# A third of the weight chunks split by DMA: a casting load, a negating copy and an accumulating load

## The chip, the cores and the metric

The kernel runs on one core of one Trainium2 chip. Its time is the device time of that core, in microseconds (us), as the median of several executions. One more execution is recorded by the hardware profiler, and all durations of single instructions come from that one.

The engines are called PE (TensorE, matrix multiplies; PEld is its weight load), DVE (VectorE), ACT (ScalarE), POOL (GpSimd) and SP (SyncE, which here only issues DMAs). Each takes its own instructions strictly in order, so an instruction that waits holds up what stands behind it. DMAs are issued from SP or POOL.

## The reference

One decoder block over 256 tokens with a model width of 2048, in float32:

```python
xn = rms_norm(h, norm_w[layer])
proj = xn @ w_in[layer]
q, k, v, z_attn, z_ssd, xbc, dt_raw, gate_logits = jnp.split(proj, split_idx, axis=-1)
...
attn = dilated_mixture_attention(q, k, v)
y_attn = (attn * jax.nn.silu(z_attn.astype(jnp.float32))).astype(x.dtype) @ w_attn_br[layer]
ssd = ssd_mixer(xbc, z_ssd, dt_raw, conv_w[layer], conv_b[layer], dt_bias[layer], ...)
y_ssd = ssd.astype(x.dtype) @ w_ssd_br[layer]
...
merged = gates[:, :, 0] * y_attn + gates[:, :, 1] * y_ssd
h = h + merged @ w_out[layer]
return rms_norm(h, final_norm_w)
```

Almost all the arithmetic is the products with the weight matrices. Every weight is read from HBM once and used for 256 tokens.

## The kernel before

A float32 product is made of products of a shorter type, float32r. A weight w is split into two float32r parts, hi = w rounded to float32r, and lo = w - hi. The activations are split in the same way. Most products are then x_hi w_hi + x_lo w_hi + x_hi w_lo: for each 128 x 128 block of weights one matmul of hi against 512 columns (both parts of 256 tokens, line 128) and one of lo against 256 columns (line 129).

The weights come in chunks of 128 partitions x 1024 columns of float32 (512 KB; those of w_v have 768 or 896 columns). The helper `weights` handles one chunk: SP issues its load into a tile `raw` (line 115), ACT makes `hi` by a copy that casts (line 116), and DVE makes `lo` by a subtraction (line 117). `raw` has five buffers, `hi` and `lo` have four each. The helper `project` (lines 120 to 130) calls it for every eight weight blocks, so a chunk is good for 16 matmuls there. `value_product` (lines 205 to 219) and the output blocks (lines 636 to 647) call it too. The last output block has a split of its own (lines 653 to 659), which also takes a `raw` buffer.

PE takes the chunks in the order of the program: values and step sizes, q and k of attention heads, the scan's streams (w_xbc, w_z), the scan's projection (w_ssd), gates (w_gate), w_attn and w_out. Between the chunks stands side work of attention and of the scan, which generators deal out (`step`, `pending`). The tile framework's scheduler sets the order on each engine. `weights` runs under `tc.high_priority`, so loads and splits are placed as early as the buffers permit: with four `hi` buffers, the cast of a chunk waits until PE is done with the chunk four before it.

POOL has little to do: squares of x at the start, constants (lines 318 and 325), one 1 MB load of decay rows for each group of the scan (line 391), residual rows (line 630) and a norm weight.

Of the kernel before, what the change touches and what calls it, by code (L numbers as in the profile page):

```python
# [13 lines left out]
F32 = mybir.dt.float32  # L14
FR = mybir.dt.float32r
# [3 lines left out]
OP = mybir.AluOpType  # L19
PSUM = bass.MemoryType.PSUM  # L20

P = 128
S = 256
# [24 lines left out]
def block_kernel(ctx: ExitStack, tc: tile.TileContext, a: dict, out: bass.AP):  # L48
    nc = tc.nc
    act, dve, pe, sp, pool = nc.scalar, nc.vector, nc.tensor, nc.sync, nc.gpsimd  # L50
# [3 lines left out]
    wts = ctx.enter_context(tc.tile_pool(name="wts", bufs=2))  # L54
# [7 lines left out]
    def ps_main():  # L62
        return ps("mm", 512, 4)
# [10 lines left out]
    def w_tile(name, cols, bufs):  # L74
        return work.tile([P, cols], F32, name=name, bufs=bufs)

    def g1():
        return w_tile("g1", 256, 4)
# [15 lines left out]
    def step(n=2):  # L94
        for _ in range(n):
            if pending:
                try:
                    next(pending[0])
                except StopIteration:
                    pending.pop(0)  # L100
# [2 lines left out]
        while pending:  # L103
            step()

    # ---- weights: load, split into two float32r parts
    def weights(src, parts=1):
        cols = src.free_size()
        with tc.high_priority(offset=100000):
            raw = wts.tile([P, 1024], F32, name="raw", bufs=5)  # L110
            hi = wts.tile([P, 1024], FR, name="hi", bufs=4)
            lo = wts.tile([P, 1024], FR, name="lo", bufs=4)
            for i in range(parts):
                c = slice(i * cols // parts, (i + 1) * cols // parts)
                sp.dma_start(raw[:, c], src[:, c])
                act.copy(hi[:, c], raw[:, c])  # L116
                dve.tensor_sub(lo[:, c], raw[:, c], hi[:, c].bitcast(F32))  # L117
        return hi, lo

    def project(src, rhs, n=KT):  # L120
        """[P channels, 2, S] in PSUM: the product is the sum of the two halves."""
        step()
        pt = ps_main()
        for k in range(n):
            if k % 8 == 0:
                hi, lo = weights(src[:, k:k + 8].rearrange("p k c -> p (k c)"))
            w = slice(k % 8 * P, (k % 8 + 1) * P)
            pe.matmul(pt, hi[:, w], rhs[:, k].rearrange("p a t -> p (a t)"), start=k == 0, stop=False)  # L128
            pe.matmul(pt[:, :S], lo[:, w], rhs[:, k, 0], start=False, stop=k == n - 1)  # L129
        return pt  # L130
# [11 lines left out]
            dve.tensor_add(dst, pt[:, :S], tmp)  # L142

    def silu_half(dst, half):
        """dst = silu(x), from half = x / 2."""
        th = g1()
        act.activation(th, half, AF.Tanh)  # L147
        dve.scalar_tensor_tensor(dst, th, 1.0, half, op0=OP.add, op1=OP.mult)
# [2 lines left out]
        act.copy(dst[:, 0], src)  # L151
        dve.tensor_sub(dst[:, 1], src, dst[:, 0].bitcast(F32))

    # ---- x * norm_w, in two float32r parts; its sum of squares over the model dimension
    with tc.high_priority(offset=100000):
        nw = small("norm_w", sp)
    ones = consts.tile([P, P], F32, name="ones")
    dve.memset(ones, 1.0)
    with tc.high_priority(offset=100000):
        first = consts.tile([P, 1], F32, name="first")  # L160
# [33 lines left out]
        dve.scalar_tensor_tensor(tmp2, tmp2, -0.5, dst, op0=OP.mult, op1=OP.mult)  # L194
        dve.scalar_tensor_tensor(dst, tmp2, 1.5, dst, op0=OP.add, op1=OP.mult)

    # ---- values: tokens on the partitions; the first head slot's carry the scan's step sizes along
    H = SSD_HEADS
    NV = NG * HD

    def apart(v):
        """Tokens in their order, seen as the even ones and the odd ones."""
        return v.rearrange("p (a h) -> p h a", h=2)

    def value_product(src, rhs, n, before=None):
# [29 lines left out]
    for t in range(2):  # L235
        pe.matmul(tot[:, t:t + 1], apart(xsq[:, 0])[:, t], ones[:, :1], start=True, stop=True)
# [4 lines left out]
    def rstd_rows():  # L241
        t = ps_tp()
        for i in range(2):
            pe.matmul(t[:, i * P:(i + 1) * P], rcol[:, i:i + 1].to_broadcast([P, P]), ident, start=True, stop=True)
        act.copy(apart(rstd), t[:, :S].rearrange("p (h a) -> p h a", h=2))
# [59 lines left out]
        act.copy(tok, t[:, :5 * H].rearrange("p (i h) -> p i h", h=H))  # L305
        yield

    # ---- the other constants
    def room(name):
        return consts.tile(list(a[name].shape), F32, name=name + "_sb")  # L310

# [2 lines left out]
    mask = consts.tile([P, 2 * 512], BF, name="mask")  # L314

    def after_start(t):
        """Nothing is loaded into t before the statistics of x are known."""
        pool.tensor_copy(t, rcol[:t.shape[0], 0:1])

    def constants():  # L320
# [9 lines left out]
        act.copy(mask, mask_f)  # L330
        yield

    # ---- rotary angles
    cosb = consts.tile([ROT, S], F32, name="cosb")
    sinb = consts.tile([ROT, S], F32, name="sinb")

# [19 lines left out]
        dve.tensor_scalar(cosb, cosb, -2.0, 1.0, op0=OP.mult, op1=OP.add)  # L356
        yield

    # ---- the scan, one group of eight heads
    sq_sum = consts.tile([P, S], F32, name="sq_sum")  # L360

    def ssd_stream(g):
        xbc = w_tile("six", 6 * S, 2).rearrange("p (i t) -> p i t", t=S)
        for i in range(6):
            ct = g * 4 + i if i < 4 else 32 + (i - 4) * GROUPS + g
            pt = project(a["w_xbc"][ct], xs)
            xc = work.tile([P, S + CONV - 1], F32, name="xc", bufs=2)
            dve.memset(xc[:, :CONV - 1], 0.0)
            evac(xc[:, CONV - 1:], pt)
            acc = g1()  # L370
            act.activation(acc, xc[:, CONV - 1:], AF.Identity, bias=conv_b[:, ct:ct + 1],  # L371
                           scale=conv_w[:, ct, CONV - 1:CONV])
            for j in range(CONV - 1):
                dve.scalar_tensor_tensor(acc, xc[:, j:j + S], conv_w[:, ct, j:j + 1], acc,  # L374
                                         op0=OP.mult, op1=OP.add)
            silu_half(xbc[:, i], acc)
        if g:
            flush()
        zs = w_tile("four", 4 * S, 1).rearrange("p (i t) -> p i t", t=S)
        for i in range(4):  # L380
            pt = project(a["w_z"][8 + g * 4 + i], xs)
            zh = g1()
            evac(zh, pt, scale=0.5)
            silu_half(zs[:, i], zh)
        return xbc, zs
# [72 lines left out]
                                     op0=OP.mult, op1=OP.subtract)  # L458
            yield

    # ---- attention, one head slot of the three groups
    swap = [(i + ROT // 2) % ROT for i in range(ROT)]

    def head_stream(h):
        src = xs if h else xu
        qk = w_tile("six", 6 * S, 2).rearrange("p (i t) -> p i t", t=S)
        waiting = []
        for g in range(NG):
            for i, base in ((g, 0), (NG + g, NG * HEADS)):
                waiting.append((qk[:, i], project(a["w_qk"][base + g * HEADS + h], src)))  # L470
                if h == 0 and len(waiting) == 1 and i == 0:
                    continue
                if h == 0 and i == NG:
                    rstd_rows()
                for dst, pt in waiting:
                    dst = dst.rearrange("p (h a) -> p h a", h=2)
                    tmp = g1()
                    act.copy(tmp, pt[:, S:])
                    if h:
                        dve.tensor_add(dst, apart(pt[:, :S]), apart(tmp))  # L480
                    else:
                        dve.tensor_add(tmp, pt[:, :S], tmp)
                        dve.tensor_mul(dst, apart(tmp), apart(rstd))
                waiting = []
        flush()
        zh = g1()
        evac(zh, project(a["w_z"][h], src), scale=0.5)
        if h == 0:
            dve.tensor_mul(zh, zh, rstd)
        za = w_tile("za", S, 1)  # L490
        silu_half(za, zh)
        v = v0 if h == 0 else values(value_product(a["w_v"][h - 1], xs, NV))
        return qk, za, v
# [44 lines left out]
        split(oT[:, h], oz)  # L538
        yield

    # ---- the SSD branch's projection, half of its inner dimension at a time
    def ssd_project(half):
        for m in range(KT):
            pt = project(a["w_ssd"][half, m], ym)
            tmp = g1()
            act.copy(tmp, pt[:, S:])
            if half:
                dve.tensor_add(ysum[:, m], ysum[:, m], tmp)
                dve.tensor_add(ysum[:, m], ysum[:, m], pt[:, :S])
            else:  # L550
                dve.tensor_add(ysum[:, m], pt[:, :S], tmp)
# [27 lines left out]
    rsqrt_mean(rs, tot2[:, :S], 2 * DM, g1(), g1())  # L579
    ssd_project(1)  # L580

    # ---- gates and merge
    for m in range(KT):
        th = []
        for br in range(2):
# [12 lines left out]
        act.mul(ym[:, m, 0], ya, 0.5)  # L598
        dve.scalar_tensor_tensor(ym[:, m, 1], ya, 0.5, ym[:, m, 0].bitcast(F32), op0=OP.mult, op1=OP.subtract)

    # ---- output projection, residual, final norm
    fw = w_tile("eight", DM, 1)
    every_row(fw, "final_norm_w")
    hres = big.tile([P, 2, DM], F32, name="hres", tag="ysum")
# [28 lines left out]
    for nb in range(NB - 1):  # L633
# [4 lines left out]
        for kk in range(KT):  # L638
            if kk % per == 0:
                hi, lo = weights(a[f"w_out{nb}"][kk // per])  # L640
# [10 lines left out]
    xres = residual(nb)  # L651
    wl = big.tile([P, 2, KT, n], FR, name="wl", tag="xs")
    for i in range(4):
        raw = wts.tile([P, 1024], F32, name="raw", bufs=5)
        sp.dma_start(raw, a[f"w_out{nb}"][i])
        k = slice(4 * i, 4 * i + 4)
        r3 = raw.rearrange("p (k c) -> p k c", k=4)
        act.copy(wl[:, 0, k], r3)
        dve.tensor_sub(wl[:, 1, k], r3, wl[:, 0, k].bitcast(F32))
# [92 lines left out]
```

## Time and profile before

| what | value |
|---|---|
| time, median of 2 runs | 1492.14 us (1491.59 to 1492.70) |
| span of the profiled execution | 1489.9 us |
| PE busy | 1472.8 us, 99% of the span |
| DVE busy | 1036.3 us, 70% |
| ACT busy | 815.6 us, 55% |
| POOL busy | 30.2 us, 2% |
| read from HBM | 275.04 MB, 186 GB/s over the span |
| share of time in which the 16 DMA engines are busy with SP's queue | 53.6% |
| splits of weight chunks on ACT and on DVE | 509 casts, 509 subtractions |

The profiled execution gives no time of its own beside its span; the span is 2.2 us under the median of the runs. A busy PE is no measure of how fast PE is, since matmuls are pipelined. It says only that PE is hardly ever without a matmul under way.

### The profile page before, as it was taken

What the parts mean: (1) busy time and instruction counts of PE and PEld (TensorE: products, weight loads), DVE (VectorE), ACT (ScalarE), POOL (GpSimd) and SP (SyncE); (2) the same over time, 40 slices, a digit from 0 to 9 for tenths busy, and PEclk for the clock granted to TensorE, in tenths of its full rate; (3) what the DMA queues carried; (4) which work ended last, traced back from release to release, by engine and by line L of the source; (5) the groups of instructions that cost most, each with busy time, mean ns of one, the idle gap of its engine ahead of it and who ended that gap; (6) DMA issues with size and microseconds to landing.
All of it is one profiled execution on the core that took longest, in us unless ns stands there. A gap on an engine that the chain in (4) does not pass through costs nothing.

```text
span 1489.9 us, 22408 instructions
## 1 busy us (share of the span) xinstructions
PE 1472.8 (99%) x8581; PEld 1295.7 (87%) x8581; DVE 1036.3 (70%) x1534; ACT 815.6 (55%) x1333; POOL 30.2 (2%) x45
## 2 busy tenths in 40 slices
PE   7999999999999999999999999999999999999997
PEld 6889888888898988888888888999988888888887
DVE  7987777978675654778888775665676666666554
ACT  6654667577544554557575644444454455555444
POOL 4000000000000000000000000000000000000000
PEclk9999999999999999999999999999999999999999
DMA  6656555655554655555555555546555555555563
GB/s 236 216 178 209 183 175 182 208 177 198 174 178 148 234 171 185 192 180 196 175 193 189 192 158 177 189 140 204 199 193 182 190 191 187 195 184 192 191 223 115
DMA packets 79004, 278.67 MB, mean 187 GB/s; under 512 B 9104, under 2 KB 9696, under 8 KB 77744
## 3 DMA queue, kind: packets, MB, share of 16 engines
q1 hardware_dynamic: 76464, 264.81, 53.6%
q0 software_dynamic: 2432, 12.43, 2.5%
q8 instruction: 67, 1.10, 0.3%
q14 instruction: 41, 0.34, 0.1%
HBM read 275.04 MB, written 2.16 MB: 186 GB/s over the span
## 4 chain that ended last, share of the span: by engine, by line
PE 97%; DVE 1%; issue 1%; DMA 0%; ACT 0%; SPq 0%; ACTq 0%; DVEq 0%
PE mm L128 52%; PE mm L129 26%; PE mm L218 3%; PE mm L216 3%; PE mm L217 3%; PE mm L646 2%; PE mm L644 2%; PE mm L645 2%; PE po L534 1%; PE sc L442 1%; DVE xw L185 1%; PE sc L513 0%; PE tp L527 0%; PE tp L407 0%; PE sc L511 0%
## 5 line engine op out<-in xcount | busy, mean ns | idle before, releaser
L128 PE MATMUL mm<-xs,hi 128*128 128x512 f32 x2576 | 911.6, 398 | 0.0
L117 DVE TENSOR_TENSOR lo<-raw,hi 128x1024 fp32r<-128x1024 f32 (+3 forms) x509 | 606.7, 1193 | 374.2 <-ACT hi L116 370.6
L116 ACT CAST hi<-raw 128x1024 fp32r<-128x1024 f32 (+3 forms) x509 | 519.0, 1021 | 501.2 <-PE mm L128 363.0
L129 PE MATMUL mm<-xs,lo 128*128 128x256 f32 x2576 | 719.4, 279 | 0.0
L128 PEld LDWEIGHTS mm<-xs,hi 128*128 128x128 f32 x2576 | 483.6, 188 | 116.1 <-ACT g L147 1.9
L129 PEld LDWEIGHTS mm<-xs,lo 128*128 128x128 f32 x2576 | 485.5, 188 | 0.0
L128 PE MATMUL mm<-ym,hi 128*128 128x512 f32 x512 | 179.8, 397 | 0.0
L129 PE MATMUL mm<-ym,lo 128*128 128x256 f32 x512 | 142.3, 278 | 0.0
L128 PEld LDWEIGHTS mm<-ym,hi 128*128 128x128 f32 x512 | 96.1, 188 | 22.1
L129 PEld LDWEIGHTS mm<-ym,lo 128*128 128x128 f32 x512 | 96.3, 188 | 0.0
L216 PE MATMUL mm<-hi,xs 128*128 128x384 f32 x224 | 75.3, 336 | 0.0
L217 PE MATMUL mm<-lo,xs 128*128 128x384 f32 x224 | 75.3, 336 | 0.0
L218 PE MATMUL mm<-hi,xs 128*128 128x384 f32 x224 | 75.3, 336 | 0.0
L374 DVE SCALAR_TENSOR_TENSOR g<-xc,conv_w_sb,g 128x256 f32<-128x256 f32 x144 | 69.5, 482 | 4.1 <-ACT g L371 1.3
L147 ACT ACTIVATE g<-g 128x256 f32<-128x256 f32 x88 | 36.5, 415 | 19.1 <-DVE g L139 12.8
L644 PE MATMUL mm<-hi,ym 128*128 128x512 f32 (+1 forms) x128 | 46.4, 363 | 0.0
L646 PE MATMUL mm<-hi,ym 128*128 128x512 f32 (+1 forms) x128 | 46.4, 363 | 0.0
L645 PE MATMUL mm<-lo,ym 128*128 128x512 f32 (+1 forms) x128 | 46.4, 362 | 0.0
L128 PE MATMUL mm<-oT,hi 128*128 128x512 f32 x128 | 45.1, 394 | 0.0
L216 PEld LDWEIGHTS mm<-hi,xs 128*128 128x128 f32 x224 | 43.5, 194 | 0.3
L217 PEld LDWEIGHTS mm<-lo,xs 128*128 128x128 f32 x224 | 43.5, 194 | 0.0
L218 PEld LDWEIGHTS mm<-hi,xs 128*128 128x128 f32 x224 | 43.5, 194 | 0.0
(226 smaller groups left out, 1324.0 us busy)
## 6 DMA issues: line engine op xcount, KB each, us to landing
raw<-w_qk SPq DMA_DIRECT2D x96, 512.0 KB, 4.3
raw<-w_xbc SPq DMA_DIRECT2D x96, 512.0 KB, 3.7
raw<-w_z SPq DMA_DIRECT2D x80, 512.0 KB, 3.8
raw<-w_ssd SPq DMA_DIRECT2D x64, 512.0 KB, 3.6
raw<-w_gate SPq DMA_DIRECT2D x64, 512.0 KB, 3.5
raw<-w_v SPq DMA_DIRECT2D x56, 384.0 KB, 3.1
raw<-w_out SPq DMA_DIRECT2D x32, 512.0 KB, 4.2
eight<-cs_rows POOLq DMA_DIRECT2D x8, 1024.0 KB, 6.8
```

Source lines behind the costliest of these rows:

```text
L116: act.copy(hi[:, c], raw[:, c])
L117: dve.tensor_sub(lo[:, c], raw[:, c], hi[:, c].bitcast(F32))
L128: pe.matmul(pt, hi[:, w], rhs[:, k].rearrange("p a t -> p (a t)"), start=k == 0, stop=False)
L129: pe.matmul(pt[:, :S], lo[:, w], rhs[:, k, 0], start=False, stop=k == n - 1)
L147: act.activation(th, half, AF.Tanh)
L216: pe.matmul(pv[t][:, :n], x_hi[:, t], hi[:, w], start=kk == 0, stop=False)
L217: pe.matmul(pv[t][:, :n], x_hi[:, t], lo[:, w], start=False, stop=False)
L218: pe.matmul(pv[t][:, :n], x_lo[:, t], hi[:, w], start=False, stop=kk == KT - 1)
L374: dve.scalar_tensor_tensor(acc, xc[:, j:j + S], conv_w[:, ct, j:j + 1], acc, op0=OP.mult, op1=OP.add)
L644: pe.matmul(po[t][:, :n], ym[:, kk, 0, tk], hi[:, w], start=kk == 0, stop=False)
L645: pe.matmul(po[t][:, :n], ym[:, kk, 0, tk], lo[:, w], start=False, stop=False)
L646: pe.matmul(po[t][:, :n], ym[:, kk, 1, tk], hi[:, w], start=False, stop=kk == KT - 1)
```

## The change

`weights` counts its calls. On every third call, if the chunk is whole (one part, 1024 columns), it takes two other tiles, `hi_acc` and `lo_acc`, of two buffers each, and makes the two parts in another way:

- POOL issues a DMA from the weights in HBM straight into `hi_acc`; the source is float32 and the destination float32r, so the DMA casts.
- ACT writes `lo_acc` = -`hi_acc`.
- POOL issues a second DMA from the same weights in HBM, which adds into `lo_acc`. The result is w - hi.

Such a chunk has no `raw` tile, no load on SP, and no instruction on DVE. Its weights are read from HBM twice. The built program has 150 such chunks: 150 loads fewer stand on SP, and 300 DMAs more on POOL. The other chunks go the old way, with three buffers instead of five for `raw`, and three instead of four for `hi` and for `lo`.

```diff
+    count = [0]
+
     def weights(src, parts=1):
         cols = src.free_size()
+        count[0] += 1
         with tc.high_priority(offset=100000):
-            raw = wts.tile([P, 1024], F32, name="raw", bufs=5)
-            hi = wts.tile([P, 1024], FR, name="hi", bufs=4)
-            lo = wts.tile([P, 1024], FR, name="lo", bufs=4)
+            if parts == 1 and cols == 1024 and count[0] % 3 == 0:
+                hi = wts.tile([P, 1024], FR, name="hi_acc", bufs=2)
+                lo = wts.tile([P, 1024], FR, name="lo_acc", bufs=2)
+                pool.dma_start(hi, src)
+                act.mul(lo, hi.bitcast(F32), -1.0)
+                pool.dma_start(lo, src, accum_op=OP.add)
+                return hi, lo
+            raw = wts.tile([P, 1024], F32, name="raw", bufs=3)
+            hi = wts.tile([P, 1024], FR, name="hi", bufs=3)
+            lo = wts.tile([P, 1024], FR, name="lo", bufs=3)
...
     for i in range(4):
-        raw = wts.tile([P, 1024], F32, name="raw", bufs=5)
+        raw = wts.tile([P, 1024], F32, name="raw", bufs=3)
```

The rest of the diff removes comments and moves line numbers by about ten: lines 115 to 117 of before are 125 to 127 of after, and the new lines are 116 (first DMA), 117 (negating copy) and 118 (accumulating DMA).

How the instructions stand now is shown at two places. The first is POOL's queue. In before, this is what POOL has left to do from the middle of the first scan groups on: the write of the decay rows to HBM and then one 1 MB load into the tile `eight` for each of the eight groups. The brackets name what a DMA waits for: DMASW is an earlier DMA of POOL, the others are engines.

```order
L297 DMA cs_rows<-four_327 64x256 [waits DMASW4_49,DVE_49]
L391 DMA eight_1932<-cs_rows 128x2048 [waits DMASW5_49,DMASW4_49]
L391 DMA eight_2592<-cs_rows 128x2048 [waits DMASW5_49,DVE_49,DMASW6_49,PE_49,Activation_49]
L391 DMA eight_3254<-cs_rows 128x2048 [waits DMASW6_49,DVE_49,DMASW7_49,PE_49,Activation_49]
L391 DMA eight_3916<-cs_rows 128x2048 [waits DMASW0_49,DVE_49,DMASW7_49,PE_49,Activation_49]
```

POOL's queue in the changed program, between the loads for the second and the third of these groups (`eight_2568` and `eight_3224` there):

```order
L116 DMA hi_acc_2660<-w_xbc 128x1024 [waits DMASW2_49,PE_49]
L118 DMA lo_acc_2661<-w_xbc 128x1024 [waits DMASW4_49,PE_49,Activation_49]
L116 DMA hi_acc_2758<-w_xbc 128x1024 [waits DMASW5_49,PE_49]
L118 DMA lo_acc_2759<-w_xbc 128x1024 [waits DMASW6_49,PE_49,Activation_49]
L116 DMA hi_acc_2877<-w_xbc 128x1024 [waits DMASW7_49,DMASW3_49,PE_49]
L118 DMA lo_acc_2878<-w_xbc 128x1024 [waits DMASW0_49,PE_49,Activation_49]
```

The two DMAs of a chunk follow each other. The first waits for PE (the release of the tile by the chunk that used it before), the second for ACT's negating copy. The first DMA of the next such chunk stands behind that second one.

The second place is ACT's queue in the same stretch of the program. Before (`g1` and `xc` are tiles of the scan's streams, `mm` a product in PSUM):

```order
L116 CAST hi_2762<-raw_2761 128x1024
L116 CAST hi_2784<-raw_2783 128x1024
L141 COPY g1_2656<-mm_2609 128x256
L116 CAST hi_2820<-raw_2819 128x1024
L371 ACTIVATE g1_2659<-xc_2654,conv_b_sb_332,conv_w_sb_331 128x256
L116 CAST hi_2842<-raw_2841 128x1024
```

And now:

```order
L117 ACTIVATE lo_acc_2759<-hi_acc_2758 128x1024
L126 CAST hi_2737<-raw_2736 128x1024
L126 CAST hi_2794<-raw_2793 128x1024
L151 COPY g1_2632<-mm_2585 128x256
L381 ACTIVATE g1_2635<-xc_2630,conv_b_sb_332,conv_w_sb_331 128x256
L157 ACTIVATE g1_2640<-g1_2635 128x256
L126 CAST hi_2816<-raw_2815 128x1024
L117 ACTIVATE lo_acc_2878<-hi_acc_2877 128x1024
```

The negating copy `lo_acc_2759` stands ahead of the cast of the chunk before it (`hi_2737`) and of a copy out of PSUM; both wait on ACT until `hi_acc_2758` has landed.

## The prediction

> **What bounds the kernel now.** I read the page's busy times and its chain of waits first, then the stages, then one stretch of PE's timeline, and last the DMAs. The page:
>
> ```profile
> PE 1472.8 (99%) x8581; PEld 1295.7 (87%) x8581; DVE 1036.3 (70%) x1534; ACT 815.6 (55%) x1333; POOL 30.2 (2%) x45
> ...
> PE 97%; DVE 1%; issue 1%; DMA 0%; ACT 0%; SPq 0%; ACTq 0%; DVEq 0%
> PE mm L128 52%; PE mm L129 26%; PE mm L218 3%; PE mm L216 3%; PE mm L217 3%; PE mm L646 2%; PE mm L644 2%; PE mm L645 2%; PE po L534 1%; PE sc L442 1%; DVE xw L185 1%; PE sc L513 0%; PE tp L527 0%; PE tp L407 0%; PE sc L511 0%
> ```
>
> The chain that ended last is PE for 97% of the span, and of that 93 points (lines 128, 129, 216 to 218, 644 to 646) are products with weight chunks. The stages (the columns are the stretch in us, its length, busy us of each engine with its count, PE's granted clock, the share of the DMA engines, GB/s) say where the rest is:
>
> ```profile
> 0.00:31.00 31.00, 22.84 (x94) 19.45 (x94) 24.31 (x35) 17.24 (x28) 16.88 (x22) 0.94 0.73 248
> ...
> 100.00:485.00 385.00, 385.00 (x2296) 337.40 (x2295) 288.75 (x462) 230.47 (x418) 2.71 (x5) 1.00 0.55 182
> ...
> 1370.00:1478.00 108.00, 108.00 (x587) 93.88 (x587) 60.59 (x73) 49.78 (x69) 2.86 (x4) 1.00 0.55 177
> 1478.00:1490.00 12.00, 3.20 (x27) 3.00 (x25) 4.12 (x16) 3.41 (x8) 0.00 (x0) 0.76 0.47 175
> ```
>
> PE lacks work only in the first 31 us (8 us of it) and in the last 12. From 100 us on it is busy without a gap at a granted clock of 1.00. The change takes no matmul away, so relieving DVE (70%) and ACT (55%) frees nothing that the end waits for. The question is only whether weight chunks still arrive in time. What keeps them in time now is seen in who waits for whom:
>
> ```profile
> DVE lo L117 <- ACT hi L116: 370.6, 328, 4.7
> ...
> ACT hi L116 <- PE mm L128: 363.0, 249, 2.7
> ```
>
> ACT's casts wait for PE to release a buffer (249 times), not for a load: the supply runs as far ahead as the four buffers let it.
>
> PE's pace, from its timeline (start, duration, matmul): two starts of line 128 eight weight blocks apart.
>
> ```profile
> 599.87 0.40 PE L128 MATMUL mm<-xs,hi 128*128 128x512 f32 x1
> ...
> 602.64 0.40 PE L128 MATMUL mm<-xs,hi 128*128 128x512 f32 x1
> ```
>
> A chunk lasts 2.77 us on PE.
>
> **The change part by part.** *Taken away:* 150 subtractions of 1.19 us and 150 casts of 1.02 us, worth nothing, because DVE and ACT do not set the end.
>
> ```profile
> L117 DVE TENSOR_TENSOR lo<-raw,hi 128x1024 fp32r<-128x1024 f32 (+3 forms) x509 | 606.7, 1193 | 374.2 <-ACT hi L116 370.6
> L116 ACT CAST hi<-raw 128x1024 fp32r<-128x1024 f32 (+3 forms) x509 | 519.0, 1021 | 501.2 <-PE mm L128 363.0
> ```
>
> and of one group of activations of the same size:
>
> ```profile
> L419 ACT ACTIVATE eight<-eight 128x1024 f32<-128x1024 f32 x8 | 8.4, 1056 | 0.0
> ```
>
> *Added on ACT:* 150 negating copies at 1.06 us (the last row above), which just replace the casts.
>
> *Added as a chain:* an accumulated chunk passes through four steps that nothing overlaps: the tile's release by PE, the first DMA, the copy, the second DMA. The time allowed for it follows from the buffers. `hi_acc` has two, and every third chunk uses one, so between PE's last matmul on a buffer and its first on the next content lie five other chunks: 5 x 2.77 = 13.9 us, and with the side work among them (97% against 93% of the chain) 13.9 x 97/93 = 14.4 us. Call this B. Let L be the chain's length. If L is under B, PE never notices. If it is over, PE stalls by s at each accumulated chunk; two such stalls lie within one chain, so L = B + 2s, and s = (L - B)/2.
>
> The trace shows no casting and no accumulating DMA. The nearest rows are POOL's plain loads and SP's (size, median us from issue to landing):
>
> ```profile
> raw<-w_xbc SPq DMA_DIRECT2D x96, 512.0 KB, 3.7
> ...
> eight<-cs_rows POOLq DMA_DIRECT2D x8, 1024.0 KB, 6.8
> ...
> cme<-x POOLq DMA_DIRECT2D x3, 512.0 KB, 5.0
> ...
> cme<-mask POOLq DMA_DIRECT2D x1, 512.0 KB, 5.8
> ```
>
> and their spread for SP's chunks and for the 1 MB load (first line `raw`, second `eight`):
>
> ```profile
> DMA to landing us min/median/max: 2.8/3.7/8.8
> ```
> ```profile
> DMA to landing us min/median/max: 5.2/6.8/9.3
> ```
>
> The first DMA moves what a 512 KB load moves: bounds 5.0 and 8.8 us, taken 5.0, the row of its own size and queue. The second must read 512 KB of weights and the 512 KB that it adds to: bounds 5.0 us (if only one read counts) and 9.3 us, the longest 1 MB load. I take 9.3, because the DMA engines get fuller. Their share now, from SP's queue between 100 and 485 us (packets, MB, share of 16 engines):
>
> ```profile
> q1 hardware_dynamic: 18724, 65.28, 51.6%
> ```
>
> 65.28 MB are 124.5 chunks of 524 KB; 0.516 x 385 us / 124.5 = 1.60 us of all 16 engines for a chunk. Three chunks last 3 x 2.77 x 97/93 = 8.7 us on PE. With two plain chunks, a casting load and an add of two reads that is 5 x 1.60 = 8.0 us of 8.7, a share of 0.92 instead of 0.55, where waits in the queues grow.
>
> For the doubled read a rule stands in the Trainium skill, "Collectives: The Full Stack", in the section on the bandwidth ceiling: an add done by DMA costs no time in the adder, but it needs two source reads on one ring, measured there as a ratio of 1.93. No row of this trace has such a DMA; at 1.93 in place of 2 the share would come to 0.91.
>
> Four hops between engines come on top. Where DVE follows ACT the timeline shows 0.03 us (a cast that ends at 602.05, its subtraction at 602.08), but a hop from PE or a DMA isn't shown alone; 0.1 each is my estimate, 0.4 in all.
>
> ```profile
> 601.00 1.05 ACT L116 CAST hi<-raw 128x1024 fp32r<-128x1024 f32 x1 [1.72 <-PE mm L128]
> ...
> 602.08 1.23 DVE L117 TENSOR_TENSOR lo<-raw,hi 128x1024 fp32r<-128x1024 f32 x1 [1.55 <-ACT hi L116]
> ```
>
> L = 5.0 + 1.06 + 9.3 + 0.4 = 15.8 us, s = (15.8 - 14.4)/2 = 0.7 us, and 150 x 0.7 = 105 us.
>
> *The wait on ACT.* The negating copy waits on ACT for the first DMA, and the cast of the plain chunk before it stands behind. This cast's chunk is due four chunks (11.1 us) after the release; first DMA 5.0, copy 1.06, cast 1.05, subtraction 1.23 and hops 0.4 make 8.7. Cover 2.4 us: nothing, as long as the first DMA lands within 7.4 us.
>
> *Fewer buffers for plain chunks.* Three `hi` buffers serve two chunks in three, so a plain chunk's buffer is released three or four chunks before it is due, as with four buffers before. Only w_v's chunks, which are never accumulated, lose one: two chunks remain as cover, against a split of three quarters of 1.02 + 1.19 us. Nothing.
>
> *Start.* Two first DMAs and, after ACT's copies, two second ones now stand ahead of or among the loads of x, and a copy stands ahead of ACT's first cast. Four times 0.52 MB at the 248 GB/s of the first stage is 8.5 us if all of it delays the loads, and nothing if it lies in gaps; the critical start is mostly DVE and its waits, so I take 5. POOL's constants wait behind the third first DMA; they are needed later.
>
> *Sum:* 1489.9 (span) + 2.2 (the median of the runs lies that much above it) + 5 + 105 = 1602 us, rounded to 1600.
>
> **The rivals.**
>
> *The chain fits (not slower).* If the second DMA takes the 1 MB load's median of 6.8 us, L is 5.0 + 1.06 + 6.8 + 0.4 = 13.3, below 14.4: no stalls, 1492 + 5 = 1497 us. It decides up to a second DMA of 8.3 us (L = 14.7, s = 0.17, 25 us, which with the start is 2%). For it speaks that each DMA price above is a median under load; against it the share of 0.92. The Trainium skill, "DMA: Bandwidth & Descriptors", section "Anatomy of one DMA", gives for a DMA issued from POOL a fixed 2.0 us plus bytes over 436 GB/s; this would make 3.2 and 4.4 us, an estimate from that page, and the chain fits with 5 us to spare. The trace's 5.0 and 6.8 us for these sizes are longer, so the page's figure is too short here.
>
> *The DMA engines become the bound.* From 8.7 us for three chunks, 4 x 1.60 us go to two plain chunks and two further units; if casting costs two plain chunks and adding three, 7 x 1.60 = 11.2 us are needed, 2.5 us too many for each of 150: 375 us, 1870 us. Nothing in the trace excludes it, as it has no such DMA. It decides from 5.4 units on.
>
> *ACT's queue starves the plain chunks.* If the first DMA takes SP's longest landing, 8.8 us, the cast behind the copy comes 1.4 us late each time: 150 x 1.4 = 210 us, 1710 us. Against it stands POOL's own 5.0.
>
> That the change doesn't do what it says is no rival: the built program has the 150 chunks. If the casting DMA did not round, `lo` would be zero, and the time the same.
>
> **How the numbers follow.** Two per cent, 30 us, is about what a measurement tells from no change. Chances: the chain a little too long (1523 to 1720 us) 0.38; it fits 0.36; DMA engines as the bound 0.16; ACT's queue 0.08; faster by over 2% 0.02, since only 8 + 9 us of the span are not PE's. Slower is 0.38 + 0.16 + 0.08 = 0.62. The range goes from 1490, as PE's work doesn't shrink, to 1820, which leaves out most of the DMA-bound case and little else.
>
> **What would show it.** If right: PE idle in front of lines 138 and 139, waiting for the DMA into `lo_acc`, some 0.7 us at each accumulated chunk; the second DMA near 9 us to landing and the first near 5; a DMA share about 0.85; DVE's busy time down by 150 x 1.19 = 179 us. It is wrong if PE has no gaps after the start (the chain fits), if the first DMA takes over 7.4 us, or if PE waits for plain `hi` or `lo`.

## The result

The changed kernel takes 1656.71 us (median of two runs, 1651.82 to 1661.61) against 1492.14 us: 1.1103 times as long, with a 95% interval of 1.1025 to 1.1182. The profiled execution has a span of 1650.0 us. The forecast was 1600 us, in a range of 1490 to 1820.

The page of the changed kernel, busy times, then DMA queues, then the chain that ended last:

```profile
PE 1527.4 (93%) x8581; PEld 1318.2 (80%) x8581; DVE 868.2 (53%) x1384; ACT 802.8 (49%) x1333; POOL 241.6 (15%) x345
...
q0 software_dynamic: 45632, 169.74, 44.4%
q1 hardware_dynamic: 54864, 186.15, 31.8%
...
issue 67%; POOL 11%; DMA 10%; PE 10%; ACT 1%; DVE 1%; POOLq 0%; SPq 0%; ACTq 0%
POOL hi_acc L116 5%; POOL lo_acc L118 5%; DMA hi_acc<-w_xbc 4%; PE mm L138 4%; DMA hi_acc<-w_z 2%; PE mm L139 2%; DMA raw<-w_v 2%; PE mm L227 1%; PE mm L228 1%; DMA hi_acc<-w_qk 1%; PE mm L226 1%; PE po L544 0%; DMA lo_acc<-w_qk 0%; DVE lo L127 0%; DMA hi_acc<-w_out 0%
```

PE has fallen from 97% of the chain to 10%. The chain now runs through POOL; "issue" is time for which the profile names no releaser. Between 600 and 650 us, where the chain holds nothing but POOL's DMAs, it is the 7.1 to 9.7 us from a first DMA to the second DMA of the same chunk, that is the landing and the copy. DVE lost 168 us of work and gained nothing for the end. The stretch from 100 to 485 us (the columns as before):

```profile
100.00:485.00 385.00, 358.20 (x2055) 307.20 (x2054) 228.18 (x396) 212.02 (x394) 54.52 (x78) 0.98 0.77 213
```

PE works off 2055 matmul records there in place of 2296, and is idle for 27 us. The loss is spread evenly. The times at which PE has started its n-th matmul, worked out from the two traces and that of a later run (three `hi_acc` buffers, below), in us:

```
matmul      350     1600     3200     4800     6400     last
before     76.1    285.8    556.1    827.9   1099.2   1480.9
after      83.6    317.9    614.9    921.0   1217.0   1641.2
f_hi3      84.1    296.1    573.4    845.2   1126.3   1508.0
```

The start costs 7.5 us; the other 153 come at a steady rate, about 1 us for each of the 150 accumulated chunks.

What PE waits for in the changed kernel, from the list of who waited for whom, is the second DMA:

```profile
PE mm L139 <- DMA lo_acc<-w_xbc: 18.8, 16, 2.7
PE mm L139 <- DMA lo_acc<-w_z: 17.9, 11, 3.6
PE mm L139 <- DMA lo_acc<-w_gate: 14.0, 14, 2.1
```

Added up over the trace, PE is idle for 114 us in gaps of over 0.15 us. 76 us of them end with the landing of a `lo_acc`, 12 us with a plain `hi` or `lo`. Waiting is not the whole loss. PE is also busy for 55 us longer with the same matmuls, and for 62 us of its busy time, in place of 4, the profile shows it at half clock (see the last section). At half speed that is at most 29 us of lost work, an estimate from these two figures.

What POOL's queue looks like when this happens (its timeline: start, duration, instruction, and in brackets the idle time before and what ended it):

```profile
615.50 0.88 POOL L118 DMA_DIRECT2D lo_acc<-w_ssd  x1 [7.58 <-ACT g L556]
616.05 0.87 POOL L116 DMA_DIRECT2D hi_acc<-w_ssd  x1
625.43 0.87 POOL L118 DMA_DIRECT2D lo_acc<-w_ssd  x1 [8.51 <-ACT lo_acc L117]
625.99 0.86 POOL L116 DMA_DIRECT2D hi_acc<-w_ssd  x1
```

and ACT's copy between them:

```profile
624.07 1.06 ACT L117 ACTIVATE lo_acc<-hi_acc 128x1024 fp32r<-128x1024 f32 x1 [4.82 <-DMA hi_acc<-w_ssd]
```

One round: the second DMA of a chunk goes out at 615.50 us, and 0.55 us later, without a wait, the first DMA of the next one. That lands after 8.0 us; the copy starts at 624.07 and ends at 625.13, and the next second DMA goes out at 625.43. A round is 9.9 us, and PE needs 8.7 for the three chunks in it. The time from issue to landing over the run (shortest, median, longest; first `hi_acc`, then `lo_acc`):

```profile
DMA to landing us min/median/max: 4.5/7.3/12.8
```
```profile
DMA to landing us min/median/max: 5.2/5.5/10.2
```

Over the 133 accumulated chunks whose buffer PE released after 100 us, worked out from the trace: the first DMA is issued 0.99 us after PE's release in the mean, and within 1 us after the previous second DMA's issue in 74% of them; landing takes 7.44, the wait for the copy 0.09, the copy 1.06, the hop to POOL 0.32, the second landing 5.98. From release to the last landing this makes 15.9 us. PE takes up the low part within 0.5 us of its landing in 53%. For 75 of the 133 chunks PE had released the tile before the previous second DMA went out, for 58 it released it later.

### The profile page after: what moved, and what is told of

Read it like the earlier page. It is cut to its first block, busy times and chain, and to the rows that moved or that the text cites. A ratio compares the mean times of both kernels' runs of the same rounds, so it can differ in the third digit from the quotient of the medians.

```text
span 1650.0 us, 22481 instructions
## 1 busy us (share of the span) xinstructions
PE 1527.4 (93%) x8581; PEld 1318.2 (80%) x8581; DVE 868.2 (53%) x1384; ACT 802.8 (49%) x1333; POOL 241.6 (15%) x345
## 4 chain that ended last, share of the span: by engine, by line
issue 67%; POOL 11%; DMA 10%; PE 10%; ACT 1%; DVE 1%; POOLq 0%; SPq 0%; ACTq 0%
POOL hi_acc L116 5%; POOL lo_acc L118 5%; DMA hi_acc<-w_xbc 4%; PE mm L138 4%; DMA hi_acc<-w_z 2%; PE mm L139 2%; DMA raw<-w_v 2%; PE mm L227 1%; PE mm L228 1%; DMA hi_acc<-w_qk 1%; PE mm L226 1%; PE po L544 0%; DMA lo_acc<-w_qk 0%; DVE lo L127 0%; DMA hi_acc<-w_out 0%
## 5 line engine op out<-in xcount | busy, mean ns | idle before, releaser
L127 DVE TENSOR_TENSOR lo<-raw,hi 128x1024 fp32r<-128x1024 f32 (+3 forms) x359 | 421.7, 1177 | 415.7 <-ACT hi L126 406.9
L138 PE MATMUL mm<-xs,hi 128*128 128x512 f32 x1704 | 608.5, 399 | 0.0
L139 PE MATMUL mm<-xs,lo 128*128 128x256 f32 x1704 | 477.7, 280 | 0.0
L126 ACT CAST hi<-raw 128x1024 fp32r<-128x1024 f32 (+3 forms) x359 | 358.1, 1002 | 156.0 <-PE mm L138 63.3
L138 PEld LDWEIGHTS mm<-xs,hi 128*128 128x128 f32 x1704 | 321.4, 189 | 76.1 <-issue 1.2
L138 PE MATMUL mm<-xs,hi_acc 128*128 128x512 f32 x872 | 323.6, 406 | 0.0
L139 PEld LDWEIGHTS mm<-xs,lo 128*128 128x128 f32 x1704 | 322.9, 189 | 0.5 <-DVE lo L127 0.3
L139 PE MATMUL mm<-xs,lo_acc 128*128 128x256 f32 x872 | 254.6, 292 | 56.8 <-DMA lo_acc<-w_xbc 18.8
L139 PEld LDWEIGHTS mm<-xs,lo_acc 128*128 128x128 f32 x872 | 169.2, 194 | 73.4 <-DMA lo_acc<-w_xbc 24.8
L138 PEld LDWEIGHTS mm<-xs,hi_acc 128*128 128x128 f32 x872 | 168.0, 193 | 38.1 <-issue 1.0
```

## The experiments

Two limits could set this pace, and in the changed kernel they lie within a microsecond of each other: the release of one of two `hi_acc` buffers by PE (the prediction's chain), and POOL's order, in which a first DMA stands behind the second DMA of the chunk before, which waits for that chunk's first landing and copy. A third theory is that the DMA engines are simply full. All ratios are to the kernel before, with 95% intervals.

**Without the dependency.** The copy reads a constant:

```diff
-                act.mul(lo, hi.bitcast(F32), -1.0)
+                act.mul(lo, ones[:, :1].to_broadcast([P, 1024]), -1.0)
```

> The changed kernel, but ACT's negating copy reads a constant of ones instead of hi_acc, so the second DMA no longer waits for the first one to land (the low part is then w - 1 and not w - hi; every DMA, copy and matmul is still there). POOL's loop: the round loses landing and copy, so it is gone: 1495 to 1530 us. DMA load: the same DMAs, so 1640 to 1665 us. Buffers: the chain gets shorter by the first landing and the copy and fits: 1495 to 1520 us.

Measured: 1502.46 us, 1.007 (1.0055 to 1.0085). Every DMA is still there:

```profile
q0 software_dynamic: 45632, 169.74, 51.3%
q1 hardware_dynamic: 54864, 186.15, 35.9%
```

The engines carry the same packets in less time, at a share of 0.87, and PE is busy for 98% of the span. DMA load is excluded as the cause. The 0.92 that the prediction feared is not far from this, and 0.87 does no harm by itself here. The run does not tell POOL's loop from the buffer chain, since both lose the first landing and the copy.

**A third buffer, first try.** `hi_acc` with three buffers, `raw` with two to make room:

```diff
-                hi = wts.tile([P, 1024], FR, name="hi_acc", bufs=2)
+                hi = wts.tile([P, 1024], FR, name="hi_acc", bufs=3)
...
-            raw = wts.tile([P, 1024], F32, name="raw", bufs=3)
+            raw = wts.tile([P, 1024], F32, name="raw", bufs=2)
```

> The changed kernel with a third buffer for hi_acc (raw gets two instead of three, to make room); POOL's order stays. Three theories. Buffers (the prediction's): the chain of an accumulated chunk starts when PE releases hi_acc. A third buffer lets it start three chunks (8.7 us) earlier, so the stalls go and the time is 1495 to 1520 us. POOL's loop: what starts the first DMA is not the release but POOL's own order, where it stands behind the second DMA of the accumulated chunk before, which itself waits for the first DMA's landing and the copy; a round is first landing 7.7 + copy 1.06 + issues and hops 1.1 = 9.9 us for every 8.7 us of PE's work, whatever the buffers: unchanged, 1640 to 1665 us. DMA load (the engines can't move more): unchanged as well, 1640 to 1665 us.

Measured: 1562.34 us, 1.0473 (1.0456 to 1.049). None of the theories named this value. Two things were wrong with the experiment. The scheduler did not keep POOL's order: with a buffer free, it placed the first DMA of the next chunk ahead of this one's second, so that buffers and order changed together. And two `raw` buffers starve the plain chunks; ACT's waits in this run:

```profile
ACT hi L126 <- DMA raw<-w_qk: 106.6, 39, 7.3
ACT hi L126 <- DMA raw<-w_ssd: 89.0, 32, 7.6
```

**The order alone.** The same tiles as in that run, and the next chunk's first DMA written ahead of the second one:

```diff
+                if nxt is not None:
+                    n_hi = wts.tile([P, 1024], FR, name="hi_acc", bufs=3)
+                    pool.dma_start(n_hi, bass.AP(tensor=a[nxt[0]].tensor, offset=nxt[1], ap=nxt[2]))
...
                 act.mul(lo, hi.bitcast(F32), -1.0)
                 pool.dma_start(lo, src, accum_op=OP.add)
```

> Tiles as in the run with three hi_acc buffers and two raw, but POOL issues the first DMA of the next accumulated chunk ahead of the second DMA of this one; the same DMAs, copies and bytes. POOL's loop: the round no longer holds first landing, copy and second issue of every chunk in a row, two chunks share it, so PE's 8.7 us for three chunks decide again: 1495 to 1530 us. DMA load: unchanged, 1640 to 1665 us. Buffers: the same time as the run with three hi_acc buffers in the old order.

Measured: 1567.30 us, 1.0503 (1.0447 to 1.0558), the same as the run before, since POOL's order is the same. It tells nothing apart, so both questions were put again.

**The third buffer, without the shortage.** `hi_acc` three, plain `lo` two, `raw` three:

```diff
-                hi = wts.tile([P, 1024], FR, name="hi_acc", bufs=2)
+                hi = wts.tile([P, 1024], FR, name="hi_acc", bufs=3)
...
-            lo = wts.tile([P, 1024], FR, name="lo", bufs=3)
+            lo = wts.tile([P, 1024], FR, name="lo", bufs=2)
```

> The changed kernel with three buffers for hi_acc; this time plain lo gives up one (two instead of three), and raw keeps its three. The scheduler then also places the first DMA of the next accumulated chunk ahead of this one's second. Buffers: first DMA starts 8.7 us earlier, so PE no longer waits for lo_acc; and if the 70 us that were left with two raw buffers were due to late plain loads, they go too: 1500 to 1520 us. If something else in the accumulated chunks costs the rest, it stays at 1555 to 1570 us.

Measured: 1517.43 us, 1.017 (1.0155 to 1.0186). Its control, in which `hi_acc` keeps two buffers:

> The changed kernel with plain lo at two buffers instead of three, hi_acc still two: the control for the two runs with three. All theories: 1645 to 1670 us, as the changed kernel. If it is faster than 1620 us, a part of the gain of the three-buffer run is not hi_acc's.

Measured: 1670.17 us, 1.1203 (1.1156 to 1.125), a little slower than the change. So the whole gain of 153 us comes with the third `hi_acc` buffer and the order that it brings. POOL's timeline in the run with three:

```profile
607.48 0.54 POOL L116 DMA_DIRECT2D hi_acc<-w_xbc  x1 [6.25 <-PE mm L139]
608.70 0.87 POOL L118 DMA_DIRECT2D lo_acc<-w_xbc  x1 [0.67 <-ACT g L556]
615.80 0.54 POOL L116 DMA_DIRECT2D hi_acc<-w_xbc  x1 [6.23 <-PE mm L139]
617.02 0.87 POOL L118 DMA_DIRECT2D lo_acc<-w_xbc  x1 [0.67 <-ACT lo_acc L117]
```

A round is 8.3 us, three chunks of 2.77, and what POOL waits for is PE's release. PE is the bound again.

**The third buffer, but the old order.** As the run with three `hi_acc` and two plain `lo` buffers, and POOL is held back by a mark that ACT makes after the copy:

```diff
+    marks = []
...
+                if marks:
+                    pool.tensor_copy(hi[:, :1], marks.pop())
                 pool.dma_start(hi, src)
                 act.mul(lo, hi.bitcast(F32), -1.0)
+                mark = work.tile([P, 1], F32, name="mark", bufs=2)
+                act.copy(mark, lo[:, :1].bitcast(F32))
+                marks.append(mark)
                 pool.dma_start(lo, src, accum_op=OP.add)
```

> Tiles as in the run with three hi_acc and two plain lo buffers, but POOL is held to the changed kernel's order: before each first DMA it copies one column into its tile from a mark that ACT makes after the negating copy of the accumulated chunk before (150 copies of one column more on ACT and on POOL), so a first DMA never starts ahead of that copy. POOL's loop: a round is again first landing 7.4, copy 1.06, issues, hops and the mark about 1.2, 9.7 us for 8.7 us of PE's work: 1620 to 1665 us. Buffers alone: the third buffer is enough, 1500 to 1525 us. If the first DMA lands in 6 us once PE's releases no longer hold it, a round is 8.3 us and the loop hides: also 1500 to 1530 us.

Measured: 1768.10 us, 1.1842 (1.1798 to 1.1887), slower than any theory said. The loop comes back although PE's release no longer holds it (in 135 of the 137 chunks whose buffer was released after 100 us, PE had released it before the previous second DMA went out):

```profile
605.79 0.87 POOL L124 DMA_DIRECT2D lo_acc<-w_ssd  x1 [28.46 <-ACT mark L122]
606.35 0.51 POOL L118 CAST hi_acc<-mark 128x1 fp32r<-128x1 f32 x1
607.15 0.55 POOL L119 DMA_DIRECT2D hi_acc<-w_ssd  x1 [0.30 <-PE mm L145]
615.81 0.87 POOL L124 DMA_DIRECT2D lo_acc<-w_ssd  x1 [8.11 <-ACT mark L122]
```

The median round is 10.9 us (worked out as above), 1.1 more than in the changed kernel; the mark's two copies and hops add 0.33 between copy and second DMA and 0.9 between the two DMAs. Without these 1.2 us a round would still be about 9.7 us, an estimate, for 8.7 us of PE's work. PE now waits for something else:

```profile
PE mm L145 <- DVE lo L133: 116.6, 59, 4.4
```

That is plain chunks, whose casts stand on ACT behind the copy that waits for the first landing: the prediction's rival of ACT's queue, read from the order and not tested by itself. PE's clock also fell: 141 us of its busy time are at half clock, against 16 us in the run with the new order. So the 1768 us are not the loop's price alone. What the run shows is that the third buffer by itself doesn't save the kernel, and that the order keeps the round too long where the release no longer matters.

**The add's second read.** The second DMA loads instead of adding:

```diff
-                pool.dma_start(lo, src, accum_op=OP.add)
+                pool.dma_start(lo, src)
```

> The changed kernel with the second DMA as a plain casting load instead of an accumulating one (the low part is then w itself). Order, waits and number of DMAs stay. POOL's loop: the round holds first landing, copy and issues; if the first DMA lands late because the add of the chunk before is still ahead of it, taking the add's second read away (1.3 to 1.6 us of all DMA engines) brings the round from 9.9 to about 8.4 us, under PE's 8.7: 1495 to 1550 us. If adding costs no more than loading, unchanged, 1640 to 1665 us.

Measured: 1527.07 us, 1.0246 (1.0209 to 1.0283). From 100 to 485 us its DMAs land like this:

```profile
hi_acc<-w_xbc POOLq DMA_DIRECT2D x16, 512.0 KB, 5.8
lo_acc<-w_xbc POOLq DMA_DIRECT2D x16, 512.0 KB, 4.6
```

In the changed kernel the same two rows read:

```profile
hi_acc<-w_xbc POOLq DMA_DIRECT2D x16, 512.0 KB, 8.1
lo_acc<-w_xbc POOLq DMA_DIRECT2D x16, 512.0 KB, 6.1
```

Without the read the second DMA lands 1.5 us sooner, and the first DMA behind it 2.3 us sooner. Not all of the latter need be the read's: the first DMA followed after 0.56 us (median after 100 us) in the changed kernel and after 1.46 us here.

**Only one of the two DMAs.** First the casting one alone, with a plain load into `raw` and DVE's subtraction for the low part:

```diff
+                raw = wts.tile([P, 1024], F32, name="raw", bufs=3)
...
+                sp.dma_start(raw, src)
                 pool.dma_start(hi, src)
-                act.mul(lo, hi.bitcast(F32), -1.0)
-                pool.dma_start(lo, src, accum_op=OP.add)
+                dve.tensor_sub(lo, raw, hi.bitcast(F32))
```

> Every third chunk's high part comes by the casting DMA from POOL; its low part the old way, from a plain load into raw and DVE's subtraction. No accumulating DMA. POOL's loop: POOL's first DMAs wait for PE's release alone, nothing stands between them: 1495 to 1520 us. If the casting DMA itself is the slow one, its landing stays near 8 us and the time may stay above 1530 us; if it was slow only because it queued behind the adds, it lands in about 5 us.

Measured: 1536.70 us, 1.0307 (1.0274 to 1.034), above the range of the loop theory. The casting DMA is not the slow one: it lands in 5.3 us (median of the run), near the 5 of the forecast, and in 5.6 to 6.7 us by tensor between 100 and 485 us. POOL waits for PE behind the low products for 1003.9 us in all, so there is no loop. For the rest the waits point at late loads into the three `raw` tiles that now serve all chunks (ACT waits 388 us and DVE 238 us for their landing, ACT 3 us in the kernel before); no run tested this.

Then the accumulating one alone, the high part by load and cast:

```diff
+                raw = wts.tile([P, 1024], F32, name="raw", bufs=3)
...
-                pool.dma_start(hi, src)
+                sp.dma_start(raw, src)
+                act.copy(hi, raw)
                 act.mul(lo, hi.bitcast(F32), -1.0)
                 pool.dma_start(lo, src, accum_op=OP.add)
```

> Every third chunk's high part is made the old way (load on SP into raw, cast on ACT), its low part by the negating copy and the accumulating DMA; POOL issues one DMA for such a chunk instead of two, the bytes are the same. POOL's loop: no first DMA stands behind a second one, so it is gone: 1495 to 1520 us in spite of 150 casts of 1.05 us more on ACT. DMA load: the same reads from HBM and the same adds, 1640 to 1665 us.

Measured: 1774.81 us, 1.1888 (1.1864 to 1.1912). Every theory missed it. The edit brought a wait of its own: the accumulated chunk's load now takes one of three `raw` tiles, and ACT waits for it:

```profile
ACT hi_acc L118 <- DMA raw<-w_xbc: 84.5, 28, 7.3
ACT hi_acc L118 <- DMA raw<-w_z: 81.9, 23, 6.3
```

To test that reading, the next run gives these loads a tile of their own (`raw_acc`, one buffer; plain `lo` two). Against the run before:

```diff
-                raw = wts.tile([P, 1024], F32, name="raw", bufs=3)
+                raw = wts.tile([P, 1024], F32, name="raw_acc", bufs=1)
```

> High part by load, cast and negating copy, low part by the accumulating DMA, as in the run that came out at 1775 us, but the accumulated chunks' loads get a tile of their own, raw_acc with one buffer, beside raw's three (plain lo has two). If that run was slow because those loads stood in the ring of three raw tiles, behind subtractions of plain chunks, the time falls to 1500 to 1540 us; if the accumulating DMA or the extra cast is what costs, it stays over 1700 us.

Measured: 1528.51 us, 1.0248 (1.0231 to 1.0265). So 246 us of that run went with the ring of three tiles. With its loads early, an accumulated chunk without the first DMA on POOL costs little, as the loop theory has it, in spite of 150 casts more. The accumulating DMA lands in 7.2 us there (median).

**Fewer accumulated chunks.**

```diff
-            if parts == 1 and cols == 1024 and count[0] % 3 == 0:
+            if parts == 1 and cols == 1024 and count[0] % 4 == 0:
```

> Every fourth chunk instead of every third. POOL's loop: a round still takes about 9.9 us, but PE now has four chunks, 11.6 us, to work off meanwhile, so the loop is hidden: 1495 to 1520 us. A cost for each accumulated chunk (DMA load, contention, clock) would go with their number: three quarters of 165 us more than before, 1600 to 1630 us.

Measured: 1514.37 us, 1.0149 (1.0132 to 1.0166). The cost does not go with the number of chunks (that would be about 1615); it nearly vanishes once a round has 11.6 us of PE's work to hide behind. The buffer chain would vanish as well: with seven chunks between two uses of a buffer it has 7 x 2.77 x 97/93 = 20.2 us. Only the two runs with three `hi_acc` and two plain `lo` buffers, in the new order and in the old, tell the loop from the release.

**The buffers alone.** No chunk is accumulated (the condition is `False`):

> No chunk is accumulated; only the buffers are those of the change (raw three instead of five, hi and lo three instead of four). All theories: 1490 to 1500 us, since two chunks of cover remain. Anything above 1510 us would mean that a part of the loss is the buffers'.

Measured: 1497.40 us, 1.0038 (1.0023 to 1.0053), 5 us more than before. In this run the three `hi` buffers serve every chunk and in the change two chunks in three, so 5 of the 165 us is the buffers' share only roughly.

No version beat the kernel before, and none could by much: PE is busy there from 31 us to the last 12 us of the span, and none of them takes a matmul away.

## Why the prediction was right or wrong

*What bounds before, and that nothing can be gained:* right. DVE fell from 1036.3 to 868.2 us of work, as forecast (179 fewer, measured 168), and no run came below 1492 us.

*The chain's length, 15.8 us:* measured 15.9, but by two errors that cancel, so this agreement is luck. The first DMA was taken at 5.0 us and landed in 7.3 (median); the second was taken at 9.3 and landed in 5.5. The doubled read was right in kind: adding in place of loading cost 1.2 us more of all 16 engines for each chunk, (0.444 x 1650.0 - 0.360 x 1521.5)/150 with the shares of POOL's queue in the changed kernel and in the run with a plain second load, whose row is

```profile
q0 software_dynamic: 45632, 169.74, 36.0%
```

The 1.60 us of the prediction for a read was somewhat too much. What it left out is that the first DMA of a chunk goes out 0.55 us behind the second DMA of the chunk before. In the run with three `hi_acc` buffers and two plain `lo` the order is reversed, and so are the landings: a median of 5.8 us for the first DMA and 7.7 for the second. Where only one of the two is issued, the casting one lands in 5.3 us and the accumulating one in 7.2. So the first DMA is late where it goes out behind an accumulating one; why that one lands sooner in the changed kernel than alone stays open.

*What starts the chain* is the step that the prediction had incomplete: it had "four steps that nothing overlaps: the tile's release by PE, the first DMA, the copy, the second DMA", with the first DMA going out at the release. In the changed kernel it is issued behind the second DMA of the chunk before, whichever comes later. The section on the change named that order in words, but the prediction priced only the release. Priced as a loop, with the measured landing, a round is 0.55 + 7.44 + 0.09 + 1.06 + 0.32 = 9.5 us; its median in the trace is 9.8. The buffer formula with the measured chain gives s = (15.9 - 14.4)/2 = 0.75 and a round of 9.4. The two can't be told apart by the changed kernel's time alone. The forecast of 105 us for 150 chunks stands against 153 measured: of the right kind, a third too small. The runs tell the two limits apart: with a third buffer and the order kept the loss stays (1768 us), with both lifted it goes (1517). So the loop is enough for a loss. Whether the release alone would cost as much, in the other order with two buffers, was not tried, and the prediction's chain is not refuted.

*The start:* 5 us taken, 7.5 measured at the 350th matmul. *Fewer buffers:* nothing taken, about 5 us measured. *Share of the DMA engines:* about 0.85 forecast, 0.77 measured between 100 and 485 us, with PE slower than forecast.

*ACT's queue:* given 0.08, priced 7.4 us of first landing as its limit. The median landing was 7.3, at that limit; DVE's waits for casts are there, but only 12 us of PE's idle time end with a plain `hi` or `lo`, against 76 with `lo_acc`. In the run with the old order forced, PE's waits for plain chunks became the larger part.

*DMA engines as the bound:* given 0.16, refuted by the run without the dependency. The Trainium skill, "DMA: Bandwidth & Descriptors", section "Anatomy of one DMA", gives 2.0 us plus bytes over 436 GB/s; for such a load this makes an estimate of 3.2 us, less than half of the 7.3 us measured. The rule of the Trainium skill, "Collectives: The Full Stack", section on the bandwidth ceiling, two reads for an add, agrees in kind: the add takes 1.2 us of all engines beside the 1.7 us of a load without it, a ratio of 1.7 where the page has 1.93. The 1.7 us are the share of POOL's queue in the run with a plain second load, less the 37 us that this queue has in the kernel before, over 300 DMAs.

## What to carry to other kernels

When a change puts a chain of two DMAs and a compute step on one in-order queue, price the round of that queue (landing of the first, step, issue of the second, issue of the next first) and not only the chain from buffer to buffer: the round limited the rate here even where a third buffer let the chain overlap with the next. A buffer more paid because it let the next item's first DMA go out ahead of this item's second; the order is to be read in the built program, since the scheduler decides it. And before moving work off an engine, read in the chain whether the end waits for that engine at all: here DVE gave up 168 us and the kernel became 165 us slower.

## What the runs showed of the hardware

A casting DMA that POOL issued 0.55 us behind an accumulating one landed in 7.3 us (median), the accumulating one in 5.5. With the order reversed, 1.2 us apart, they took 5.8 and 7.7. Each in a run without the other of the pair, they took 5.3 and 7.2. So the casting DMA took 2.0 us longer behind an accumulating one than alone, and the accumulating one 0.5 us longer behind a casting one. The other load on the DMA engines differs between these runs.

The casting load costs little or nothing beside a plain one: in the run with only casting DMAs it landed in 4.2 to 5.5 us by tensor over the whole run (5.6 to 6.7 between 100 and 485 us), when SP's plain loads of the same size took 5.1 to 5.5.

The clock that PE is granted fell in the changed kernel, from a mean of 0.997 to

```profile
core 0: 1650.0 us, clock 0.979
```

Between 100 us and the last stage, the records show half clock in fourteen stretches that the kernel before hasn't, thirteen of 3.4 us and one of 10.2. In them a 512-column matmul starts every 0.43 us in place of 0.23. Eight begin within 1.3 us after PE had been idle for 2.0 to 3.6 us, one during an idle time of 2.4 us, and four at two shorter gaps of 0.5 to 1.2 us; before the one of 10.2 us the records show only a gap of 0.5 us. What these stretches add to the time was not measured by itself; the estimate in the section on the result, at most 29 us, takes in the start and the end too.
